# Stores of layer 1's preparation moved from the SP queue to the POOL queue in a two-layer decoder step

## Chip, cores and metric

The kernel runs on one core of a Trainium2 chip. The metric is the device time of one execution in microseconds; the median of three runs is given. The core has a matrix engine (TensorE, "PE" in the profile, with its weight loads as "PEld"), a vector engine (VectorE, "DVE"), a scalar engine (ScalarE, "ACT"), a general engine (GpSimd, "POOL") and a sequencer for transfers (SyncE, "SP"). Transfers run on 16 DMA engines.

## What is computed

One inference step of a two-layer decoder trunk over 1024 prompt rows and 8 x 4 sample rows (1056 columns of 1024 features). Layer 0 has a state-space branch and an HGRN2 branch. Layer 1, the one that the change touches, is RWKV-7 time mixing:

```python
xr, xw, xk, xv, xa, xg = (xn + xx * mix[m] for m in range(6))
r = xr @ wp[0]; k = xk @ wp[1]; v = xv @ wp[2]; z = xg @ wp[3]
decay = exp(-DECAY_SCALE * sigmoid(w0 + tanh(xw @ w1) @ w2))
a = sigmoid(a0 + (xa @ a1) @ a2)
g = sigmoid(xg @ g1) @ g2
kk = normalised heads of k * k_k;  k = k * (1 + (a - 1) * k_a)
# per head, token after token:
s = s * w_t - (s @ kk_t) outer (kk_t * a_t) + v_t outer k_t;  y_t = s @ r_t
out = (groupnorm(y) + bonus) * g * silu(z);  h = h + out @ w_o
```

A last RMSNorm gives the output.

## The kernel before

The columns are worked on in two halves (512 prompt columns; 512 prompt columns and 32 sample columns), features in eight blocks of 128 partitions ("pairs" of two heads). All dense products split their float32 operands into a high and a low part (`split`, L70 and L72) and run three matmuls per product (`dense2`, L805).

Layer 1 of one half goes through these steps. `l1_first` makes k, r and v (and, in `lora_second`, sw and a), block after block, and stores each to HBM (tensors kd, rd, vd, swd, ad; v also in chunks of 64 tokens, vc). `rwkv_ready` drives the preparation of the eight pairs: `rwkv_pre` loads k, sw and a of a pair, scans, and makes the operands ZB, which it stores to zr and bk; `rwkv_r` loads r, completes zr and stores rk; `rwkv_mask` makes masked products of the operands and stores them to nd; after four pairs `rwkv_inverse` loads nd back as sN in another layout, solves 31 steps on VectorE in the tile sX, and stores the inverses to xd and, transposed, to xnd. `l1_gate` makes the gates and `gates` stores two factors (g1, g2) by chunk. Then `chains` goes through 32 batches (two halves, eight chunks of 64 tokens, two groups of four pairs): `batch_load` loads BK, ZR, v, DT (from xd) and DA (from xnd), and `batch_products` (L1514), `batch_below` (L1548), `batch_block` (L1560) and the following steps compute; `rwkv_tail` loads the gates, and `l1_out` makes the output projection.

Nearly every transfer of the kernel is issued through the helper `dma` (L52), that is, on SP, loads and stores in one order. The generators above are interleaved by the rates in `run`; the order of the instructions on each engine's queue is then set, when the kernel is built, by a planner that places each instruction by priority and by estimated costs. Each engine, SP and POOL among them, works through its queue in that order. ZB, sN and sX have one buffer each. POOL's own work in these steps is small: the first column of each chunk in ZB (L1344), products for the samples (L1366), the clearing of sX ahead of an inverse (L1399), and parts of the normalisation (L857 to L863) and of the splits (L979, L980).

Of the kernel before, what the change touches and what calls it, by code (L numbers as in the profile page):

```python
# [25 lines left out]
NP = 4  # L26
# [10 lines left out]
class Builder:  # L37
# [12 lines left out]

    def dma(self, out, in_):
        self.nc.sync.dma_start(out, in_)  # L52

    def lnexp(self, after):

        with self.tc.issue_after(after.ins):
            self.nc.scalar.preload_act_table_set("natural_log_exp_and_others")
# [978 lines left out]
    def l1_first(self, hf):  # L1036

        nc, I, V, A = self.nc, self.I, self.nc.vector, self.nc.scalar
        c0, n, cuts = HALF[hf]
        cs = slice(c0, c0 + n)  # L1040

        lo = self.evt("lora")
        parts = self.lora_weights((("w", 1), ("a", 4)))
        xs = self.plain(hf), self.difference(hf)

        def first(ps, q0, q):
            A.activation(lo[0:64, q0:q0 + q], ps[0:64], AF.Tanh)
            A.activation(lo[64:128, q0:q0 + q], ps[64:128], AF.Copy)

        self.dense2(list(zip(parts, xs)), cuts, first)  # L1050
        yield

        wa = self.pair(n)
        for x, h, l in ((wa[0], slice(0, 64), slice(64, 128)), (wa[1], slice(64, 128), slice(0, 64))):
            A.activation(x[h, :n], lo[h, :n], AF.Copy)
            V.tensor_tensor(out=x[l, :n], in0=lo[h, :n], in1=x[h, :n].bitcast(F32), op=ALU.subtract)
        early = 0 if hf else self.ahead
        ready = self.rwkv_ready(hf, early)
        for j, m, dst, name in ((1, 2, self.k_d, "k"), (0, 0, self.r_d, "r"), (2, 3, self.v_d, "v")):
            self.wpool = self.wp8[hf][name]  # L1060
            self.evto = self.ev8[hf]
            xs = self.mixed(hf, m)
            for t in range(KT):
                while name == "k" and t > 3 and self.ah is None:
                    yield
                w = self.weights2(I["rw_w_rkvz"][0, j, :, 128 * t:128 * t + 128], KT)
                ev = self.evt()
                self.dense2([(w, xs)], cuts, lambda ps, q0, q: self.evac(ev[:, q0:q0 + q], ps, q, self.evto), last=t == KT - 1)
                self.dma(dst[t][:, cs], ev[:, :n])
                if name == "v":  # L1070
                    self.dma(self.vc_d[hf][t // NP][:, :, t % NP], ev[:, 0:512].rearrange("p (c t) -> p c t", t=64))
                if name == "k":
                    self.key_sums(hf, t, ev[:, :n])
                    if t == 3:
                        self.key_norms(hf)
                    elif t > 3 and early:
                        next(ready)
                else:
                    with self.tc.high_priority(offset=0):
                        next(ready, None)  # L1080
                if name == "v":
                    self.made["v"][hf] += 1
                yield
                if name == "k":
                    for i in range(2):
                        if t == self.lt[i]:
                            yield from self.lora_second(hf, wa, 4 * i)

    def lora_second(self, hf, wa, m0):

        nc, I, A = self.nc, self.I, self.nc.scalar
        c0, n, cuts = HALF[hf]
        cs = slice(c0, c0 + n)
        fs = slice(128 * m0, 128 * m0 + 512)
        wh, wl = self.weights2([I[x][0][:, fs] for x in ("rw_w2", "rw_a2")], KT)
        for m in range(4):
            both = [(slice(r0, r0 + 64), 4 * i + m, bias, dst, name, self.evt()) for i, r0, bias, dst, name in
                    ((0, 0, self.w0, self.sw_d, "sw"), (1, 64, self.a0, self.a_d, "aa"))]
            for q0, q in cuts:
                pss = [x[:, :q] for x in (self.bank(), self.PS(512))]  # L1100
                for x, ps, (rs, k, *_) in zip(wa, pss, both):
                    nc.tensor.matmul(ps, wh[:, k], x[:, q0:q0 + q], start=True, stop=False)
                for x, ps, (rs, k, *_) in zip(wa, pss, both):
                    nc.tensor.matmul(ps, wl[rs, k], x[rs, q0:q0 + q], start=False, stop=True)
                for ps, (rs, k, bias, dst, name, ev) in zip(pss, both):
                    A.activation(ev[:, q0:q0 + q], ps, AF.Sigmoid, bias=bias[:, m0 + m:m0 + m + 1])  # L1106
            for rs, k, bias, dst, name, ev in both:
                self.dma(dst[m0 + m][:, cs], ev[:, :n])
            if (m0 + m) % self.ly == self.ly - 1:
                yield  # L1110

# [69 lines left out]
    def gates(self, hf, p, g):  # L1181


        V, A = self.nc.vector, self.nc.scalar
        c0, n, cuts = HALF[hf]
        bon, v = (self.stage(x, 544)[:, :n] for x in ("ek", "es"))
        for t, d in ((bon, self.rk_d), (v, self.v_d)):
            self.dma(t, d[p][:, c0:c0 + n])
        self.within(n, cuts, bon, self.blkr, lambda cs, ps: V.tensor_tensor(out=v[:, cs], in0=v[:, cs], in1=ps, op=ALU.mult))
        V.scalar_tensor_tensor(out=v, in0=v, scalar=self.rwv["ln_b"][:, p:p + 1], in1=g, op0=ALU.add, op1=ALU.mult)  # L1190
        A.activation(bon, g, AF.Copy, scale=self.rwv["ln_w"][:, p:p + 1])
        for t, d, ds in ((bon, self.g1_d, self.g1s_d), (v, self.g2_d, self.g2s_d)):
            self.dma(d[hf][:, :, p], t[:, 0:512].rearrange("p (c t) -> p c t", t=64))
            if hf:
                self.dma(ds[:, p], t[:, 512:544])


    def rwkv_constants(self, kp):
# [96 lines left out]
    def rwkv_pre(self, hf, p, ahead=False):  # L1295
# [8 lines left out]
        c0, n, cuts = HALF[hf]  # L1304
        gs = slice(c0, c0 + n)
# [7 lines left out]
        ZB = T("ZB", 8, 3, 64)  # L1313
# [3 lines left out]
        for q0, q in cuts:  # L1317
            cs = slice(q0, q0 + q)
# [9 lines left out]
        P = sw  # L1328
# [12 lines left out]
        for x, d, z in ((pr(t1), pr(P), ZB[:, :, 0]),) + (((sm(t1), sm(P), sm3(SM[:, 0])),) if hf else ()):  # L1341
            c = x.shape[2]
# [4 lines left out]
        A.activation(a, a, AF.Identity, scale=c1(W["k_a"]), bias=c1(self.omka))  # L1347
        V.tensor_tensor(out=k, in0=k, in1=a, op=ALU.mult)
        both(V, k, t3, ZB[:, :, 2], 4)
        self.dma(self.zr_d[hf][p // NP][:, :, p % NP, 0], ZB[:, :, 0])  # L1350

        bk = self.bk_d[hf][p // NP][:, :, p % NP]
        self.dma(bk[0:64], ZB[0:64, :, 1:3])
        for i in range(2):
            self.dma(bk[64:128, :, i], ZB[64:128, :, 2 - i])
        return (p, ZB, a), (p, k, P)

    def rwkv_r(self, hf, p, k, P):

        V, G = self.nc.vector, self.nc.gpsimd  # L1360
        c0, n, cuts = HALF[hf]
        gs = slice(c0, c0 + n)
        r = self.stage("er", 544)[:, :n]
        self.dma(r, self.r_d[p][:, gs])
        if hf:
            G.tensor_tensor(out=self.SM[p][:, 1], in0=r[:, 512:544], in1=P[:, 512:544], op=ALU.mult)  # L1366
        V.tensor_tensor(out=P[:, 0:512], in0=r[:, 0:512], in1=P[:, 0:512], op=ALU.mult)
        self.dma(self.zr_d[hf][p // NP][:, :, p % NP, 1], P[:, 0:512].rearrange("p (c t) -> p c t", t=64))
        V.scalar_tensor_tensor(out=r, in0=r, scalar=self.rwv["r_k"][:, p:p + 1], in1=k, op0=ALU.mult, op1=ALU.mult)
        self.dma(self.rk_d[p][:, gs], r)  # L1370

    def rwkv_mask(self, hf, p, ZB, t1):

        nc, V = self.nc, self.nc.vector
        ps = self.PS(8, 32)
        for c in range(8):
            for i in range(2):
                js = slice(32 * i, 32 * i + 32)
                for h in range(2):
                    o, hr = 64 * h + 32 * i, slice(64 * h, 64 * h + 64)  # L1380
                    nc.tensor.matmul(ps[o:o + 32, c], ZB[hr, c, 1, js], ZB[hr, c, 0, js], start=True, stop=True)
        Nt = t1[:, 0:256].rearrange("p (c t) -> p c t", t=32)
        V.tensor_tensor(out=Nt, in0=ps, in1=self.cmd[:].unsqueeze(1).broadcast_to([128, 8, 32]), op=ALU.mult)
        self.dma(self.n_d[hf][p // NP][:, :, p % NP], Nt)

    def blocks(self, d, i, h):

# [3 lines left out]
    def rwkv_inverse(self, hf, b):  # L1391
# [3 lines left out]
        N, X = T("sN", 32, 32), T("sX", 32, 32)  # L1395
# [8 lines left out]
        with self.tc.high_priority(offset=0):  # L1404
            for j in range(31):
                n = 31 - j
                for E, t, s0, s1 in groups:
                    m = min(j + 1, s1) - s0
# [4 lines left out]
                for E, t, s0, s1 in groups:  # L1413
                    m = min(j + 1, s1) - s0
# [1 line left out]
                        w = t[:, 0:m * n].rearrange("p (s t) -> p s t", t=n)  # L1416
                        E.tensor_tensor(out=X[:, s0:s0 + m, j + 1:32], in0=X[:, s0:s0 + m, j + 1:32], in1=w, op=ALU.subtract)  # L1417
        for i, h, q in quarters:
            self.dma(self.blocks(self.x_d[hf][b][:, :, :, 32 * i:32 * i + 32], i, h), X[q])
        Xn = T("sN", 32, 32)  # L1420
        A.activation(Xn[:64], X[:64].rearrange("q s t -> q t s"), AF.Copy)
        for h in range(2):
            self.dma(self.xn_d[hf][b][:, h].rearrange("t c p s -> (c p) t s"), Xn[32 * h:32 * h + 32])

    def chains(self):

# [587 lines left out]
```

## Time and profile before

| what | us |
|---|---|
| median of three runs | 1889.67 |
| lowest, highest | 1886.45, 1898.71 |
| the profiled execution, its own time | 1892.82 |
| its span in the profile | 1891.1 |
| TensorE busy | 1706.0 |
| VectorE busy | 1297.9 |
| ScalarE busy | 977.1 |
| POOL busy | 140.7 |

The span goes from the first to the last instruction; the execution's own time is a little longer. Busy times count computing instructions alone; what an engine spends on issuing a transfer appears in the timeline of its queue ("SPq"). A row of a wait names the waiting instruction by its line and the tile that it makes, and what ended the wait.

### The profile page before, as it was taken

The numbers are of one execution on the slowest core, as the hardware profiler recorded it, in microseconds if no ns is written. First come the engines' busy times: TensorE is split into PE (matmuls) and PEld (weight loads), VectorE is DVE, ScalarE is ACT, GpSimd is POOL, SyncE is SP. The second block draws the span as 40 slices with busy tenths as digits, with TensorE's granted clock in tenths as the row PEclk, the third lists the DMA queues.
The fourth block names the chain that finished last, engine by engine and source line by source line (L and its number), as shares of the span: only waits on it lengthen the run. The fifth ranks groups of instructions, "written<-read, shape, count | busy, mean of one in ns | idle before, by whom it ended". The sixth has DMA issues, their size and how long they took to land. (4 is left out here: it accounts for less than half of the span.)

```text
span 1891.1 us, 39586 instructions
## 1 busy us (share of the span) xinstructions
PE 1706.0 (90%) x15060; PEld 1419.1 (75%) x15060; DVE 1297.9 (69%) x3010; ACT 977.1 (52%) x1886; POOL 140.7 (7%) x257
## 2 busy tenths in 40 slices
PE   4999989999997698997399999998899999999867
PEld 3877868988876576775377778887798887788756
DVE  5797798875678624789598734868968566565554
ACT  5445555555645334643356766645555435434454
POOL 1210011000004200011021000000000000000000
PEclk9899999888999797998599889989898998999799
DMA  8555554444562556699758234589794666453453
GB/s 205 173 157 141 136 149 130 138 131 123 172 186 84 173 184 200 185 255 262 194 141 203 81 125 161 146 226 243 206 220 120 178 159 166 126 157 104 118 157 106
DMA packets 555010, 308.39 MB, mean 163 GB/s; under 512 B 284883, under 2 KB 489043, under 8 KB 554820
## 3 DMA queue, kind: packets, MB, share of 16 engines
q1 hardware_dynamic: 554820, 305.86, 59.1%
q8 instruction: 119, 1.95, 0.4%
q14 instruction: 71, 0.58, 0.1%
HBM read 199.76 MB, written 104.81 MB: 161 GB/s over the span
## 5 line engine op out<-in xcount | busy, mean ns | idle before, releaser
L805 PE MATMUL dps<-xh,wh 128*128 128x272 f32 (+3 forms) x1696 | 581.2, 349 | 55.3 <-ACT xh L70 22.3
L805 PE MATMUL dps<-xl,wh 128*128 128x272 f32 (+3 forms) x1696 | 582.6, 346 | 18.7 <-DVE xl L72 18.1
L805 PE MATMUL dps<-xh,wl 128*128 128x272 f32 (+3 forms) x1696 | 575.3, 342 | 4.8 <-DVE wl L72 4.7
L805 PEld LDWEIGHTS dps<-xh,wh 128*128 128x128 f32 x1696 | 330.9, 198 | 108.2 <-ACT xh L70 27.0
L805 PEld LDWEIGHTS dps<-xl,wh 128*128 128x128 f32 x1696 | 334.5, 198 | 60.9 <-DVE xl L72 28.1
L805 PEld LDWEIGHTS dps<-xh,wl 128*128 128x128 f32 x1696 | 335.0, 198 | 37.7 <-DVE wl L72 8.4
L70 ACT ACTIVATE wh<-ws 128x512 fp32r<-128x512 f32 (+1 forms) x336 | 195.9, 619 | 289.9 <-PE dps L805 198.8
L72 DVE TENSOR_TENSOR wl<-ws,wh 128x512 fp32r<-128x512 f32 (+1 forms) x336 | 224.1, 685 | 97.6 <-ACT wh L70 96.7
L1514 PE MATMUL m<-ZR,BK 64*128 64x128 f32 x512 | 62.8, 296 | 21.4 <-DMA ZR<-zr 20.6
L1514 PEld LDWEIGHTS m<-ZR,BK 64*128 64x128 f32 x512 | 54.0, 196 | 28.7 <-issue 14.3
L70 ACT ACTIVATE xh<-mm 128x256 fp32r<-128x256 f32 (+1 forms) x112 | 52.8, 481 | 37.5 <-DVE mm L929 19.7
L72 DVE TENSOR_TENSOR xl<-mm,xh 128x256 fp32r<-128x256 f32 (+1 forms) x112 | 55.6, 507 | 5.6 <-ACT xh L70 2.6
L805 PE MATMUL dps<-gh,wh 128*128 128x272 f32 (+1 forms) x176 | 55.8, 317 | 2.1 <-ACT ev L1106 1.1
L805 PE MATMUL dps<-gl,wh 128*128 128x272 f32 (+1 forms) x176 | 54.8, 312 | 1.4 <-DVE gl L72 1.4
L805 PE MATMUL dps<-gh,wl 128*128 128x272 f32 (+1 forms) x176 | 54.5, 310 | 0.1
L1411 DVE TENSOR_TENSOR sT<-sX,sN 128x31 f32<-128x31 f32 (+15 forms) x124 | 42.1, 339 | 11.9 <-DMA sN<-nd 10.2
L66 DVE COPY ev<-dps 128x272 f32<-128x272 f32 (+1 forms) x43 | 22.5, 526 | 40.2 <-PE dps L805 35.0
L64 ACT ACTIVATE ev<-dps 128x272 f32<-128x272 f32 (+1 forms) x65 | 29.3, 450 | 37.5 <-PE dps L805 37.1
L1571 PE MATMUL m<-ZM,DT 64*64 64x128 f32 x512 | 41.1, 291 | 2.4 <-DVE MR L1517 2.4
L1417 DVE TENSOR_TENSOR sX<-sX,sT 128x31 f32<-128x31 f32 (+15 forms) x124 | 42.0, 339 | 1.7
L863 POOL COPY edge<-h 128x1 f32<-128x1 f32 x8 | 27.1, 3392 | 182.6 <-DVE h L850 182.5
L805 PEld LDWEIGHTS dps<-gh,wh 128*128 128x128 f32 x176 | 35.1, 199 | 6.3 <-ACT ev L1106 1.6
(644 smaller groups left out, 3365.1 us busy)
## 6 DMA issues: line engine op xcount, KB each, us to landing
ws<-in_rw_w_rkvz SPq DMA_DIRECT2D x128, 256.0 KB, 4.2
ws<-in_even_w_in SPq DMA_DIRECT2D x96, 256.0 KB, 3.7
ws<-in_rw_w_o SPq DMA_DIRECT2D x48, 256.0 KB, 3.1
ws<-in_even_w_out SPq DMA_DIRECT2D x32, 256.0 KB, 3.8
BK<-bk SPq DMA_DIRECT2D x32, 256.0 KB, 4.4
ZR<-zr SPq DMA_DIRECT2D x32, 256.0 KB, 2.7
pr<-ev SPq DMA_DIRECT2D x20, 272.0 KB, 2.0
pr<-ev SPq DMA_DIRECT2D x20, 256.0 KB, 3.9
```

The source lines that it names most:

```text
L64: return self.nc.scalar.activation(out, in_, AF.Copy)
L66: return self.nc.vector.tensor_copy(out, in_)
L70: self.nc.scalar.activation(hi, x, AF.Copy)
L72: e.tensor_tensor(out=lo, in0=x, in1=hi.bitcast(F32), op=ALU.subtract)
L805: mm = lambda c0, n, i, u, k, v: self.nc.tensor.matmul(ps[c0], u[:, k, :], v[:, c0:c0 + n], start=i == 0, stop=i == len(terms) - 1)
L863: G.tensor_copy(self.edge[:, k:k + 1], x[:, 512:513])
L1411: E.tensor_tensor(out=w, in0=X[:, s0:s0 + m, j:j + 1].broadcast_to([128, m, n]), in1=N[:, j, j + 1:32].unsqueeze(1).broadcast_to([128, m, ...
L1417: E.tensor_tensor(out=X[:, s0:s0 + m, j + 1:32], in0=X[:, s0:s0 + m, j + 1:32], in1=w, op=ALU.subtract)
L1514: nc.tensor.matmul(f2(pm[h][:, q]), f2(BK[hr, q]), f2(ZR[hr, q]), start=True, stop=True)
L1571: nc.tensor.matmul(pd[hr, q], DT[hr, q], ZM[hr, q], start=True, stop=True)
```

## The change

A second helper, `store`, issues a transfer from POOL instead of SP. The stores of layer 1's preparation call it: k, r, v, sw and a, the chunks of v, the gates, zr, bk, rk, nd, xd and xnd. Loads, the chains' output and layer 0 stay with `dma`.

```diff
     def dma(self, out, in_):
         self.nc.sync.dma_start(out, in_)
+
+    def store(self, out, in_):
+
+        self.nc.gpsimd.dma_start(out, in_)
...
-                self.dma(dst[t][:, cs], ev[:, :n])
+                self.store(dst[t][:, cs], ev[:, :n])
                 if name == "v":
-                    self.dma(self.vc_d[hf][t // NP][:, :, t % NP], ev[:, 0:512].rearrange("p (c t) -> p c t", t=64))
+                    self.store(self.vc_d[hf][t // NP][:, :, t % NP], ev[:, 0:512].rearrange("p (c t) -> p c t", t=64))
...
             for rs, k, bias, dst, name, ev in both:
-                self.dma(dst[m0 + m][:, cs], ev[:, :n])
+                self.store(dst[m0 + m][:, cs], ev[:, :n])
...
         for t, d, ds in ((bon, self.g1_d, self.g1s_d), (v, self.g2_d, self.g2s_d)):
-            self.dma(d[hf][:, :, p], t[:, 0:512].rearrange("p (c t) -> p c t", t=64))
+            self.store(d[hf][:, :, p], t[:, 0:512].rearrange("p (c t) -> p c t", t=64))
             if hf:
-                self.dma(ds[:, p], t[:, 512:544])
+                self.store(ds[:, p], t[:, 512:544])
...
-        self.dma(self.zr_d[hf][p // NP][:, :, p % NP, 0], ZB[:, :, 0])
+        self.store(self.zr_d[hf][p // NP][:, :, p % NP, 0], ZB[:, :, 0])
 
         bk = self.bk_d[hf][p // NP][:, :, p % NP]
-        self.dma(bk[0:64], ZB[0:64, :, 1:3])
+        self.store(bk[0:64], ZB[0:64, :, 1:3])
         for i in range(2):
-            self.dma(bk[64:128, :, i], ZB[64:128, :, 2 - i])
+            self.store(bk[64:128, :, i], ZB[64:128, :, 2 - i])
...
-        self.dma(self.zr_d[hf][p // NP][:, :, p % NP, 1], P[:, 0:512].rearrange("p (c t) -> p c t", t=64))
+        self.store(self.zr_d[hf][p // NP][:, :, p % NP, 1], P[:, 0:512].rearrange("p (c t) -> p c t", t=64))
...
-        self.dma(self.rk_d[p][:, gs], r)
+        self.store(self.rk_d[p][:, gs], r)
...
-        self.dma(self.n_d[hf][p // NP][:, :, p % NP], Nt)
+        self.store(self.n_d[hf][p // NP][:, :, p % NP], Nt)
...
         for i, h, q in quarters:
-            self.dma(self.blocks(self.x_d[hf][b][:, :, :, 32 * i:32 * i + 32], i, h), X[q])
+            self.store(self.blocks(self.x_d[hf][b][:, :, :, 32 * i:32 * i + 32], i, h), X[q])
...
         for h in range(2):
-            self.dma(self.xn_d[hf][b][:, h].rearrange("t c p s -> (c p) t s"), Xn[32 * h:32 * h + 32])
+            self.store(self.xn_d[hf][b][:, h].rearrange("t c p s -> (c p) t s"), Xn[32 * h:32 * h + 32])
```

## Rows read from the trace of the kernel before

**Rows 1.** The page, busy time, share and instructions of each engine.
```profile
PE 1706.0 (90%) x15060; PEld 1419.1 (75%) x15060; DVE 1297.9 (69%) x3010; ACT 977.1 (52%) x1886; POOL 140.7 (7%) x257
```

**Rows 2.** Stretches: PE, PEld, DVE, ACT, POOL busy us; PE clock, DMA share, GB/s.
```profile
850.00:900.00 50.00, 37.97 (x261) 26.66 (x260) 45.26 (x101) 19.80 (x32) 7.86 (x14) 0.83 1.02 266
900.00:950.00 50.00, 22.21 (x235) 17.71 (x236) 30.86 (x68) 16.03 (x37) 1.11 (x2) 0.55 0.72 171
...
1300.00:1350.00 50.00, 41.51 (x586) 35.56 (x586) 49.03 (x131) 31.53 (x77) 2.75 (x6) 0.94 0.74 204
1350.00:1400.00 50.00, 50.00 (x536) 46.66 (x536) 31.90 (x81) 19.18 (x37) 4.10 (x5) 0.96 1.00 237
```

**Rows 3.** PE's timeline, 893 to 945 us: start, us, what, idle before, releaser.
```profile
903.80 3.06 PE L1514 MATMUL m<-ZR,BK 64*128 64x128 f32 x16 [9.71 <-DMA ZR<-zr]
...
919.61 0.81 PE L1548 MATMUL m<-DA,MZ 32*32 32x32 f32 x16 [8.62 <-DMA DA<-xnd]
...
932.61 3.06 PE L1514 MATMUL m<-ZR,BK 64*128 64x128 f32 x16 [10.87 <-DMA ZR<-zr]
```

**Rows 4.** SP's timeline, 889 to 918 us: start, us of issuing, what.
```profile
889.08 0.53 SPq L52 DMA_DIRECT2D bk<-ZB  x1
...
891.87 1.20 SPq L52 DMA_DIRECT2D bk<-ZB  x2
893.17 2.26 SPq L52 DMA_DIRECT2D nd<-ea  x1
...
898.01 0.42 SPq L52 DMA_DIRECT2D ZR<-zr  x1
...
899.96 4.90 SPq L52 DMA_DIRECT2D xd<-sX  x3
...
908.15 0.50 SPq L52 DMA_DIRECT2D xnd<-sN  x1
...
916.88 0.99 SPq L52 DMA_DIRECT2D DA<-xnd  x2
```

**Rows 5.** DMA issues from 850 to 900 us: count, KB each, median us to landing.
```profile
vc<-ev SPq DMA_DIRECT2D x7, 256.0 KB
vd<-ev SPq DMA_DIRECT2D x6, 256.0 KB, 3.7
...
bk<-ZB SPq DMA_DIRECT2D x6, 128.0 KB, 3.4
bk<-ZB SPq DMA_DIRECT2D x3, 256.0 KB, 4.5
zr<-es SPq DMA_DIRECT2D x2, 256.0 KB
rkd<-er SPq DMA_DIRECT2D x2, 256.0 KB
...
zr<-ZB SPq DMA_DIRECT2D x2, 256.0 KB, 3.4
...
nd<-ea SPq DMA_DIRECT2D x3, 128.0 KB, 4.5
...
xd<-sX SPq DMA_DIRECT2D x1, 128.0 KB
```

**Rows 6.** Issues by tensor over the run: ns of one, min/median/max; first and last.
```profile
L52 SPq DMA_DIRECT2D kd<-ev x16: 319/338/712, 652.2 to 1191.1; - x16
...
L52 SPq DMA_DIRECT2D zr<-ZB x16: 519/530/979, 746.5 to 1359.0; - x16
```

**Rows 7.** POOL's groups: busy us, mean ns of one; idle before them, releasers.
```profile
L863 POOL COPY edge<-h 128x1 f32<-128x1 f32 x8 | 27.1, 3392 | 182.6 <-DVE h L850 182.5
L199 POOL COPY us<-ev 128x512 f32<-128x512 f32 x8 | 10.8, 1364 | 57.3 <-DVE ev L66 26.1 <-ACT ev L64 25.3 <-DVE ep L256 3.9
L1344 POOL COPY ZB<-e 128x8 f32<-128x8 f32 x16 | 8.5, 529 | 273.2 <-DVE e L1322 183.8 <-DMA bk<-ZB 20.6 <-DMA nd<-ea 19.6
```

**Rows 8.** POOL's clearing of sX: ns of one, min/median/max.
```profile
L1399 POOL MEMSET sX<- x4: 952/953/954, 640.3 to 1385.1; 128x1024 f32 x4
```

## The prediction

> **What bounds the kernel now.** I read the page's busy shares first, then the stretches of layer 1, then the waits of TensorE, then SP's own timeline, and last POOL's rows. TensorE is busy for 1706.0 of 1891.1 us, POOL for 140.7 [rows 1]. So a change that computes nothing can win only the time in which TensorE stands still, 185 us in all, and only the part of it that hangs on the moved stores. The stretches say where that is [rows 2]: from 850 to 900 us TensorE is idle for 12.0 us and from 900 to 950 for 27.8, at a granted clock of 0.83 and 0.55; from 1300 to 1350 it is idle for 8.5. Those are the places where the preparation of a half of layer 1 ends and the chains begin (first half) or run beside it (second half). In 850 to 900 and in 1350 to 1400 the 16 DMA engines are busy all the time (1.02 and 1.00), so there it is not SP alone that is late.
>
> The three long idles of TensorE in the first of these places are named by the trace [rows 3]: 9.71 us until the chains' first ZR load lands, 8.62 until DA lands, 10.87 until a ZR load of the second group lands; together 29.20. SP's own timeline [rows 4] shows what stood ahead of these loads. SP works one instruction after another, and from 889 to 917 it has hardly a gap: the ZR load is issued at 898.01 behind bk stores of 0.53 and 1.20 us (this one two stores) and an nd store of 2.26; the inverse's four xd stores go out from 899.96, the second xnd store at 908.15, and the DA load that needs it at 916.88, with zr, bk and rkd stores in between.
>
> **The change part by part.** *Removed from SP.* The diff moves 280 stores. By their access patterns 112 go out in 128 pieces, one per partition (k, r, v, sw, a: 80; rk: 16; the samples' gates: 16), 48 in 512 (bk), and 120 in 1024 (zr 32, gates 32, vc 16, nd 16, xd 16, xnd 8). The median issue on SP was 0.338 us for the first kind and 0.530 for the last [rows 6], so SP gets back about 112 x 0.338 + 168 x 0.530 = 127 us, spread over 650 to 1570 us. TensorE is covered by its own work nearly everywhere there, so I cost this at nothing except at the three idles:
> - first ZR load: bk 0.53 + 1.20 and nd 2.26 = 3.99 us stood right ahead of it; minus 4.0.
> - DA load: 8.7 us pass between the second xnd store and DA's issue; the moved stores among them leave, but xnd must still land before DA goes, and xd and xnd themselves become dearer (below). Of the 8.62 I take 2.5 back.
> - second ZR load: it waits for a zr store whose data are late themselves; SP is free for the er load ahead of that. I take 2.
>
> Of the 8.5 us in the second half, where chains and dense products both feed TensorE, I take 1.5. Sum: minus 10.
>
> *Added on POOL.* The trace shows no store issued by POOL, so its price is bounded by rows. The lower end is what SP needs for the same store, 0.53 us [rows 6]. How POOL makes the list of a store's pieces no row shows; if it goes through them one by one, its own work per element is the nearer row: a MEMSET of 1024 columns takes 0.953 us [rows 8], a COPY of 512 columns 1.364, so 2.7 for 1024 [rows 7]; the upper end that I can reason for is the 3.4 us to which a tiny COPY was stretched [rows 7], on top of the 0.5. I take the middle between MEMSET and COPY, 1.8 us for 1024 pieces, as 0.6 fixed and 1.2 for the pieces: 1.2 us for 512 and 0.75 for 128. In all 120 x 1.8 + 48 x 1.2 + 112 x 0.75 = 358 us of POOL, on an engine that is idle for long spells ahead of its ZB copies (273.2 us in all) [rows 7]. The tight stretch is 850 to 900: 32 moved stores [rows 5], 15 of 1024 pieces, 9 of 512, 8 of 128, together 27.0 + 10.8 + 6.0 = 43.8 us, and POOL's own 7.9 [rows 2]: 51.7 in 50. POOL just keeps up, each store some 1 to 3 us later than SP had it done.
>
> *Who waits for that.* POOL runs in order too. Behind a store that waits for its data stand POOL's ZB copies, the SM products and the clearing of X ahead of an inverse; behind the ZB copy stand the mask matmuls and the next stores; and VectorE can't write ZB for the next pair until bk has landed. The idle ahead of the ZB copies covers a microsecond or two per pair; if it is gone, VectorE stops, and with it the weight splits that TensorE needs. The four xd and two xnd stores cost 6 x 1.8 = 10.8 us where SP took from 899.96 to 908.65, 8.7; that is plus 2 at the DA load, which with the gain above is why I take only 2.5 there. For the rest I take plus 2.
>
> Sum: minus 10 plus 2 = minus 8 against the profiled execution's own 1892.82. That one is 3.15 above the median of the three runs, so the forecast is 1889.67 - 8 = 1882. The order of the instructions on each engine is planned anew when an instruction changes engine, so a few microseconds either way belong to the result whatever the stores do.
>
> The trace shows POOL's work stretched by its neighbour: a COPY of one column takes 3.4 us on average at one place [rows 7]. The Trainium skill (SBUF — State Buffer, section "SBUF: two separate sides") goes further: an issue on POOL writes its list through ports that VectorE can lock, and the DMA then waits; by it the queue on POOL would be the dearer one. But POOL's write-only MEMSET takes 952 to 954 ns in all four places [rows 8], so I give that rule a small chance, below. The same skill (DMA: Bandwidth & Descriptors, section "Latency and other measured facts") prices the first byte at about 1 us from POOL and 0.6 from SP; by that each step store-to-load is 0.4 later and the sum would be minus 7.
>
> **The rivals.**
> *A. SP's queue was all of it.* If POOL's store costs 1 us or less for 1024 pieces, nothing is late on POOL, and loads no longer stand behind stores. Then most of the 29.20 us goes, say 22, and 6 of the 8.5 in the second half: 1889.67 - 28 = 1862. For it: SP without a gap at the very place [rows 4]. Against it: the DMA engines are full there [rows 2], and a load that leaves SP sooner still waits for them.
>
> *B. POOL becomes the bound: slower.* The stretch of 850 to 900 decides. 15 x 1024 + 9 x 512 + 8 x 128 is 20.5 times 1024 pieces; with 0.6 fixed, 32 x 0.6 + 20.5 b = 50 - 7.9 gives b = 1.1, so from about 1.7 us per store of 1024 pieces on POOL runs behind (the forecast's 1.8 by 2 us, 2.4 by 14). At 3.9 (0.8 + 3.1 b) the stretch holds 32 x 0.8 + 20.5 x 3.1 = 89 us of stores, 39 too many; X, zr and xnd go out that much later, TensorE has nothing else there (27.8 us idle already), and the time is 1889.67 + 40 = 1930. For it: the COPY's 2.7 us lies well over the point from which this decides [rows 7]. Against it: MEMSET's 0.953 [rows 8].
>
> *C. The ports starve POOL.* If each of the 32 stores is stretched to 3.4 us more, as the COPY was, that is 109 us in 50 us: 60 late, 1950. This is the skill's rule worked out in rows; against it stands rows 8.
>
> *D. Nothing happens.* The DMA engines carry the same bytes, and they are the wall at 1.02 [rows 2]: 1890. The Trainium skill says so in general (DMA: Bandwidth & Descriptors, section "Issuing engines are not separate DMA queues"): only the time to issue is saved.
>
> **How the numbers follow.** Chances: forecast 0.36, A 0.29, B 0.25, C 0.06, D 0.04. A measurement of this kernel tells about 1% (19 us) from no change. The forecast's own range is 1870 to 1905; of its 0.36, 0.05 lies below 1871 and 0.03 above 1908. Of A 0.26 is faster by over 1%, of B 0.24 slower, C is slower, D within. Together faster 0.31, within 1% 0.36, slower 0.33. The range goes from 1852 (leaves 0.05 of A out) to 1945 (leaves C and 0.07 of B out). Cases of both signs hold most of the chance, so the likeliest one's range stands beside it: 1870 to 1905.
>
> **What would show it.** Right: POOL's store of 1024 pieces between 1.4 and 2.2 us; TensorE's three idles down from 29 to some 20 us; SP with gaps between 890 and 917. A shows as a price under 1 us and idles under 10 us. B shows as POOL without a gap from 850 to 930, ZB waits on VectorE for bk, and an idle of 30 us or more before the first DA or ZR; C as the same with store times that vary with VectorE's work. D shows as SP free, DMA engines at 1.0, idles as before. I am wrong in the mechanism if the idles change little and the time moves by over 1% elsewhere, for example in the gate stage or by another order of TensorE's work.

## The result and the profile after

The changed kernel is slightly slower: 1911.08 us median of 11 executions (1895.85 to 1919.15) against 1897.55 of 11 of the kernel before. The ratio on record, which here and below is not simply that of the two medians, is 1.0064 (95% interval 1.0038 to 1.0090). Measured once more on another occasion it was 1.0072 (1.0037 to 1.0106). The forecast was 1882, slightly faster. The profiled execution of the changed kernel took 1911.55 us, its span is 1909.8, 18.7 us more than before. Of these TensorE is busy for 12.3 more, with the same instructions, and idle for 6.4 more; the granted clock of the profiled executions is 0.900 on average, 0.911 before.

POOL did what the diff says: 280 more instructions, and a queue of its own. First the page of the changed kernel, busy times [rows 1] and queues (packets, MB, share of the 16 engines):

```profile
PE 1718.3 (90%) x15060; PEld 1430.2 (75%) x15060; DVE 1302.0 (68%) x3010; ACT 979.4 (51%) x1888; POOL 345.0 (18%) x537
...
q1 hardware_dynamic: 388548, 245.02, 45.3%
q0 software_dynamic: 19328, 60.84, 11.7%
```

The price of a store on POOL, ns of one (min/median/max), first and last start [rows 6 had SP's]:

```profile
L56 POOL DMA_DIRECT2D kd<-ev x16: 542/542/753, 654.4 to 1211.0; - x16
L56 POOL DMA_DIRECT2D bk<-ZB x48: 649/687/1264, 751.0 to 1397.8; - x48
L56 POOL DMA_DIRECT2D zr<-ZB x16: 847/865/1125, 749.2 to 1393.5; - x16
L56 POOL DMA_DIRECT2D xd<-sX x16: 786/790/817, 903.7 to 1490.2; - x16
```

So the median is 0.54 to 0.63 us for 128 pieces (0.63 for the samples' gates alone), 0.69 for 512 and 0.79 to 0.91 for 1024. All of them together are 345.0 - 140.7 = 204 us, and POOL is nowhere full. The stretches, in the columns of [rows 2]:

```profile
850.00:900.00 50.00, 43.52 (x350) 31.98 (x348) 45.61 (x100) 18.53 (x32) 32.40 (x44) 0.89 0.92 273
900.00:950.00 50.00, 20.33 (x223) 16.97 (x224) 31.13 (x78) 17.89 (x39) 12.99 (x18) 0.53 0.75 195
1300.00:1350.00 50.00, 46.24 (x604) 40.91 (x603) 44.51 (x115) 30.40 (x75) 15.42 (x24) 0.86 0.79 218
```

TensorE idles 6.5 us instead of 12.0 in the first of them, 29.7 instead of 27.8 in the second, and 3.8 instead of 8.5 in the third. Its three idles at the chains' start [rows 3] are now

```profile
902.16 3.06 PE L1518 MATMUL m<-ZR,BK 64*128 64x128 f32 x16 [3.00 <-DMA ZR<-zr]
...
920.94 0.28 PE L1552 MATMUL m<-DA,MZ 32*32 32x32 f32 x2 [6.00 <-DMA DA<-xnd]
...
933.61 3.06 PE L1518 MATMUL m<-ZR,BK 64*128 64x128 f32 x16 [10.03 <-DMA ZR<-zr]
```

together 19.03 us instead of 29.20: 10.2 less, where the forecast's three parts took 8.5 off them. (The other 14 of the DA matmuls wait for 0.42 more.) Yet the time is longer. What is late in these stretches is the stores themselves; DMA issues of the changed kernel from 850 to 900 us, median us to landing in the last column [rows 5]:

```profile
vd<-ev POOLq DMA_DIRECT2D x6, 256.0 KB, 6.3
...
zr<-ZB POOLq DMA_DIRECT2D x3, 256.0 KB, 6.3
bk<-ZB POOLq DMA_DIRECT2D x6, 128.0 KB, 7.3
...
nd<-ea POOLq DMA_DIRECT2D x3, 128.0 KB, 7.5
```

From SP these took 3.7, 3.4, 3.4 and 4.5 us. And something else has changed that the diff does not name: with the stores on another engine the planner ordered every engine anew. Of the program's 10,805 matmuls (15,060 instructions in the profile's count) 4,129 stand at another place than before, of ScalarE's 1,742 operations 696, of VectorE's 3,010 operations 1,236.

### The profile page after: what moved, and what is told of

It is laid out like the page before. It is cut to its first block, busy times and chain, and to the rows that moved or that the text cites. A ratio compares the mean times of both kernels' runs of the same rounds, so it can differ in the third digit from the quotient of the medians.

```text
span 1909.8 us, 39764 instructions
## 1 busy us (share of the span) xinstructions
PE 1718.3 (90%) x15060; PEld 1430.2 (75%) x15060; DVE 1302.0 (68%) x3010; ACT 979.4 (51%) x1888; POOL 345.0 (18%) x537
## 3 DMA queue, kind: packets, MB, share of 16 engines
q1 hardware_dynamic: 388548, 245.02, 45.3%
q0 software_dynamic: 19328, 60.84, 11.7%
## 5 line engine op out<-in xcount | busy, mean ns | idle before, releaser
L809 PE MATMUL dps<-xh,wh 128*128 128x272 f32 (+3 forms) x1696 | 580.4, 349 | 57.1 <-ACT xh L74 19.4
L1518 PE MATMUL m<-ZR,BK 64*128 64x128 f32 x512 | 67.4, 308 | 13.0 <-DMA ZR<-zr 13.0
L68 ACT ACTIVATE ev<-dps 128x272 f32<-128x272 f32 (+1 forms) x65 | 29.2, 451 | 37.3 <-PE dps L809 33.0
L1415 DVE TENSOR_TENSOR sT<-sX,sN 128x31 f32<-128x31 f32 (+15 forms) x124 | 41.9, 338 | 8.6 <-DMA sN<-nd 6.8
L1421 DVE TENSOR_TENSOR sX<-sX,sT 128x31 f32<-128x31 f32 (+15 forms) x124 | 41.9, 338 | 2.3 <-DVE sT L1415 0.4
L56 POOL DMA_DIRECT2D kd<-ev x16 | 8.9, 558 | 178.3 <-ACT ev L68 60.8
```

The costliest lines, as they stand in the source:

```text
L68: return self.nc.scalar.activation(out, in_, AF.Copy)
L809: mm = lambda c0, n, i, u, k, v: self.nc.tensor.matmul(ps[c0], u[:, k, :], v[:, c0:c0 + n], start=i == 0, stop=i == len(terms) - 1)
L1415: E.tensor_tensor(out=w, in0=X[:, s0:s0 + m, j:j + 1].broadcast_to([128, m, n]), in1=N[:, j, j + 1:32].unsqueeze(1).broadcast_to([128, m, ...
L1518: nc.tensor.matmul(f2(pm[h][:, q]), f2(BK[hr, q]), f2(ZR[hr, q]), start=True, stop=True)
```

## The experiments

Two theories remained: the **queue** (stores on POOL land later, and buffers and loads wait for them) and the **order** (the new plan makes TensorE wait elsewhere). A third, **scatter**, had to be watched: executions of one kernel differ by over 1%, and the granted clock goes with it. The first two can be taken apart, since a program's instructions are recorded in the same sequence whatever issues the stores. The kernel is recorded twice; the planned order of the first recording is laid on the second by edges that fix only the order of issue on an engine and wait for nothing (lines of e1's kernel):

```diff
     def store(self, out, in_):
-        self.nc.gpsimd.dma_start(out, in_)
+        (self.nc.gpsimd if self.on_pool else self.nc.sync).dma_start(out, in_)
...
+def follow(tc, order):
+
+    place = {n: k for k, n in enumerate(order)}
+    mine = {}
+    for i in tc.nc.cur_bb.bb.instructions:
+        if i.name in place and str(i.engine).split(".")[-1] in ('PE', 'Activation', 'DVE', 'Pool', 'SP'):
+            mine.setdefault(i.engine, []).append(i)
+    info = mybir.DependencyInfo(mybir.DependencyClass.NoSync, mybir.DependencyReason.DATA)
+    for ins in mine.values():
+        ins.sort(key=lambda i: place[i.name])
+        for a, b in zip(ins, ins[1:]):
+            tc.add_manual_dep(b, a.name, info, reason="order")
...
+    traced(first, inputs, False)
+    nc = bacc.Bacc("TRN2", target_bir_lowering=False, num_devices=1)
+    arrays = traced(nc, inputs, True, order_of(first))
```

All ratios are to the kernel before on the same chip; each is from 10 to 12 executions.

| run | order | issued by POOL | ratio (95% interval) |
|---|---|---|---|
| changed kernel | new | all 280 | 1.0064 (1.0038, 1.0090) |
| e14 (again) | new | all 280 | 1.0072 (1.0037, 1.0106) |
| e2 | new | none | 1.0059 (1.0027, 1.0092) |
| e1 | old | all 280 | 1.0044 (1.0016, 1.0071) |
| e12 (e1 again) | old | all 280 | 1.0001 (0.9970, 1.0032) |
| e4 | old | all but gates | 1.0005 (0.9984, 1.0025) |
| e7 | old | all but inverses | 1.0006 (0.9979, 1.0033) |
| e10 | old | all but both | 0.9970 (0.9943, 0.9997) |
| e15 (e10 again) | old | all but both | 1.0001 (0.9977, 1.0024) |
| e11 | old | gates and inverses | 0.9995 (0.9962, 1.0027) |
| e5 | old | gates | 1.0000 (0.9971, 1.0029) |
| e3 | planned for it | the 16 of rk | 1.0000 (0.9970, 1.0030) |
| e6 | new, one place edited | all 280 | 1.0012 (0.9986, 1.0038) |
| e13 | new, two places edited | all 280 | 1.0035 (1.0003, 1.0067) |
| e9 | new, one place edited | all but gates | 0.9983 (0.9955, 1.0010) |
| e8 | new, one place edited | none | 1.0032 (1.0009, 1.0055) |
| e16 | old, the same place spoiled | none | 1.0027 (1.0000, 1.0054) |

**e1, e2: the queue with the old order, the order with the old queue.**

> The stores are on POOL's queue as in the changed kernel, but every engine is held to the order of instructions that the kernel before has (its 10,805 matmuls, 1,742 ScalarE and 3,010 VectorE operations, and SP's loads). Queue theory (the time is lost because stores on a second queue land later, and the buffers and loads behind them are late): the ratio to before stays at 1.004 to 1.010, as the changed kernel's. Order theory (the time is lost because all instructions were planned anew when the stores changed their engine, and the new order makes TensorE wait elsewhere; the queue itself costs nothing and gives the 7 us at the chains' start): the loss is gone, ratio 0.994 to 1.000, and TensorE's idles at the chains' start are some 22 us or less instead of 29.

> The stores are on SP's queue as in the kernel before, but every engine is held to the order of instructions that the changed kernel has. Queue theory: the loss goes with the POOL queue, ratio 0.996 to 1.002. Order theory: the loss stays and the gain at the chains' start is missing, ratio 1.006 to 1.013, with an idle of about 5 us of TensorE at about 754 us behind ScalarE's exponentials, as in the changed kernel.

Both lost: 1.0044 and 1.0059. The second is, but for 0.0001, what the order theory asked for: with every store on SP and only the order changed, nearly the whole loss is there, and so is the idle behind ScalarE:

```profile
763.52 0.79 PE L810 MATMUL dps<-xh,wh 128*128 128x512 f32 x1 [5.22 <-ACT ev L1111]
```

The first seemed to say that the queue costs too, so the next runs looked for that.

**e3: another replanning.**

> Of all the stores only the 16 of the sums r (16 of 280 moved ones, small) are issued by POOL, in an order planned anew: 3,213 of the 10,805 matmuls stand at another place than before. Queue theory: 16 stores of 280 cost at most a twentieth of the loss, ratio 0.998 to 1.002. Order theory: any replanning can move the time by half a per cent either way, so a ratio as far from 1 as 0.993 or 1.008 would not surprise, and one within 0.998 to 1.002 would say that a replanning alone does not cost.

1.0000. A replanning that moves nearly a third of the matmuls need not cost anything; so it is this plan that costs, not replanning as such.

**e4, e5, e7, e10, e11: parts of the queue, old order.** The edit is `self.dma` instead of `self.store` in the lines of the stores that stay on SP; e4 for instance:

```diff
-            self.store(d[hf][:, :, p], t[:, 0:512].rearrange("p (c t) -> p c t", t=64))
+            self.dma(d[hf][:, :, p], t[:, 0:512].rearrange("p (c t) -> p c t", t=64))
             if hf:
-                self.store(ds[:, p], t[:, 512:544])
+                self.dma(ds[:, p], t[:, 512:544])
```

> All stores but the gates' 48 are issued by POOL, and every engine is held to the order of the kernel before. Gate theory (in the run with every store on POOL and the old order the gates' buffer came back later, so that ScalarE waited 2.9 us instead of 0.3 for the load of r*k at 960 to 1010 us, TensorE idled 3.9 us behind it, and its clock fell to 1.2 GHz): that wait is 0.3 to 1 us again, and with the shorter idles at the chains' start the ratio to before is 0.994 to 0.999. Landing theory (every store on the second queue lands later and what is lost is spread over the kernel): ratio 1.002 to 1.006. Scatter theory (the granted clock falls after any small idle, wherever it is): 0.998 to 1.004.

> Only the gates' 48 stores are issued by POOL, and every engine is held to the order of the kernel before. Gate theory: the wait for the load of r*k at 960 to 1010 us is 2 to 3 us, the idles at the chains' start are the 29 us of before, ratio 1.003 to 1.007. Landing theory: these stores are a sixth of those moved, ratio 1.000 to 1.002. Scatter theory: 0.998 to 1.003.

The wait named there behaves as the gate theory says, the time does not. Waits of ScalarE from 960 to 1015 us (us in total, times, longest), in e1, e4 and e5, and in e2:

```profile
ACT e L75 <- DMA ek<-rkd: 2.9, 3, 2.1
```

```profile
ACT e L75 <- DMA ek<-rkd: 0.3, 1, 0.3
```

```profile
ACT e L75 <- DMA ek<-rkd: 2.9, 2, 1.6
```

```profile
ACT e L75 <- DMA ek<-rkd: 5.7, 2, 4.7
```

With the gates alone on POOL the wait is 2.9 us as in e1, and costs nothing (1.0000). With every store on SP but the new order it is 5.7 us: in the changed kernel, which has 6.6, it comes from the order, not from the queue. The gate theory falls.

> Order of the kernel before on every engine; all stores issued by POOL, the gates' too, but for the 24 of the inverses (xd, xnd), which SP issues. Crowd theory (with every store on POOL the inverses' six stores leave at 986 to 991 us, 9 us earlier than from SP, while the gates' stores, their loads and the weights are under way; all then land late, and ScalarE waits for the load of r*k): without the inverses in the second queue the gates' stores come back in time, ratio 0.998 to 1.002, and ScalarE's wait for the load of r*k at 960 to 1015 us is under 1.5 us. Gate theory (gates' stores behind other stores of POOL are enough): ratio 1.003 to 1.006 and the wait 2 to 3 us. Scatter theory: 1.000 to 1.004.

e7: 1.0006. The crowd theory expected that, but the wait that it was to remove is 3.1 us: a miss in the mechanism.

> Order of the kernel before; POOL issues the operands of the chains (k, r, v, the decays, the masked products, their sums), while SP issues the gates and the inverses. Crowd theory (the loss with every store on POOL needs the gates and the inverses together on the second queue): at most what either alone gave back, ratio 0.997 to 1.001, with the three idles at the chains' start near 19 us. Landing theory (all stores on the second queue cost): 1.001 to 1.004. Scatter theory: 0.998 to 1.002 here, and the same for the two runs beside it.

> Order of the kernel before; POOL issues only the gates and the inverses, the other way round. Crowd theory: these two together cost by themselves what the whole queue cost with this order, and nothing is gained at the chains' start beyond what the inverses' earlier leaving gives: ratio 1.003 to 1.007. Landing theory: 1.000 to 1.003. Scatter theory: 0.998 to 1.002.

> Every store on POOL in the order of the kernel before, as in the first of these experiments (there 1.0044, interval 1.0016 to 1.0071), measured once more beside its two halves on one chip. If the loss is the queue's: 1.003 to 1.006 again. If the first measurement caught the granted clock low by chance: 0.998 to 1.002, as the runs without the gates or without the inverses, and then the queue as a whole costs and gives nothing that can be measured.

e10, e11 and e12: 0.9970, 0.9995, 1.0001. The crowd theory falls with e11. e12, the same kernel as e1 measured again on another chip, loses nothing; the two average 1.0022, and their intervals overlap. The executions of e1 had a mean granted clock of 0.9009, those of e12 of 0.9046 (the kernel before 0.9064 and 0.9063 beside them), and between executions of one kernel 0.001 of clock goes with 1.3 us (fitted over all runs of the study), so some 5 of the 8 us between the two means go with the clock. What lowered it in e1 is not known. The six measurements with the old order in which POOL issues the chains' operands (e1, e4, e7, e10, e12, e15) have a mean ratio of 1.0005. With the new order the queue makes as little difference: 1.0064 and 1.0072 on POOL, 1.0059 on SP. So the queue neither costs nor gives anything that can be measured here, which is to say about 0.2%. Nor do the edges themselves: e5 and e11 carry them at 1.0000 and 0.9995.

**e6, e8, e16: one place in ScalarE's order.** The clearest new idle of the changed kernel is at 755 us, long before the chains. ScalarE of the kernel before:

```profile
752.53 0.67 ACT L1106 ACTIVATE ev<-dps,w 128x512 f32<-128x512 f32 x1
753.22 1.28 ACT L1329 ACT_TABLE_LOAD   x1
754.51 0.63 ACT L1329 ACTIVATE as<-e 128x512 f32<-128x512 f32 x1
```

and of the changed kernel:

```profile
754.85 1.28 ACT L1333 ACT_TABLE_LOAD   x1
756.15 0.63 ACT L1333 ACTIVATE as<-e 128x512 f32<-128x512 f32 x1
756.81 0.63 ACT L1334 ACTIVATE e<-e 128x512 f32<-128x512 f32 x1
757.35 0.20 ACT L1335 ACTIVATE PC<-as 128x8 f32<-128x8 f32 x1
757.56 1.28 ACT L1110 ACT_TABLE_LOAD   x1
758.86 0.69 ACT L1110 ACTIVATE ev<-dps,w 128x512 f32<-128x512 f32 x1
```

The sigmoid that empties the bank of sums into which TensorE wants to write next (`lora_second`, the row with `ev<-dps,w`) stood ahead of the exponentials of `rwkv_pre`; now two exponentials, a small copy and two loads of a function table stand ahead of it. TensorE of the kernel before, of the changed one, of e6 and of e16 (start, us, what, idle before):

```profile
740.47 0.80 PE L1102 MATMUL dps<-xh,wh 128*128 128x512 f32 x1 [1.07 <-ACT ev L1106]
753.25 0.79 PE L805 MATMUL dps<-xh,wh 128*128 128x512 f32 x1 [1.09 <-ACT ev L1106]
```

```profile
742.67 0.79 PE L1106 MATMUL dps<-xh,wh 128*128 128x512 f32 x1 [1.07 <-ACT ev L1110]
...
759.60 0.80 PE L809 MATMUL dps<-xh,wh 128*128 128x512 f32 x1 [5.23 <-ACT ev L1110]
```

```profile
742.61 0.80 PE L1107 MATMUL dps<-xh,wh 128*128 128x512 f32 x1 [1.07 <-ACT ev L1111]
755.40 0.79 PE L810 MATMUL dps<-xh,wh 128*128 128x512 f32 x1 [1.09 <-ACT ev L1111]
```

```profile
742.47 0.80 PE L1107 MATMUL dps<-xh,wh 128*128 128x512 f32 x1 [1.07 <-ACT ev L1111]
759.58 0.80 PE L810 MATMUL dps<-xh,wh 128*128 128x512 f32 x1 [5.42 <-ACT ev L1111]
```

Between the same two matmuls 12.78 us pass in the kernel before, 16.93 in the changed kernel, 12.79 in e6 and 17.11 in e16. In e6 three instructions have moved in the new order, in e16 the same three in the old one, the other way. The edit of e6 (e8 and e9 have the same):

```diff
+EXPS, EVACS = ["I-8001", "I-8002", "I-8003"], ["I-7787", "I-7788"]
+
+
+def edited(order):
+
+    rest = [n for n in order if n not in EXPS]
+    b = rest.index(EVACS[-1])
+    return rest[:b + 1] + EXPS + rest[b + 1:]
```

> The changed kernel with its own order on every engine, but for three ScalarE instructions at about 755 us (two exponentials and a copy of 8 columns), which stand behind the two sigmoids that follow them instead of ahead of them. Order theory: TensorE's idle of 5.2 us there falls to about 1 us, and the time is 4 us (and some clock) below the changed kernel's: ratio to before 1.002 to 1.005. If ScalarE's order here is worth nothing, because what follows waits for the same stores: 1.006 to 1.007, as the changed kernel.

> All stores on SP as in the kernel before, the changed kernel's order on every engine, but for the three ScalarE instructions at about 755 us, which stand behind the two sigmoids. Order theory: the same swap gives back on SP what it gave on POOL (there 1.0064 became 1.0012), so the 1.0059 of the run with this order and all stores on SP becomes 1.000 to 1.003. If the swap's gain on POOL was of the POOL queue (the sigmoids' buffers wait for stores there): 1.004 to 1.007.

> The kernel before, all stores on SP and its own order on every engine, but for the three ScalarE instructions at about 755 us, which stand ahead of the two sigmoids as in the changed kernel's order. Order theory: TensorE idles about 5 us there instead of 1, the stretch that took 30.0 us takes 33 to 35 us, and the ratio to before is 1.002 to 1.005. If the place is worth its idle alone or less, because the chains' start 130 us later waits for SP's backlog all the same: the stretch takes 33 to 35 us and the ratio is 0.999 to 1.002.

e6: 1.0012, beside 1.0064 and 1.0072 without the edit; a little below the 1.002 expected. e8: 1.0032, beside e2's 1.0059; a little above the 1.003 expected. e16: 1.0027, as expected, though its interval (1.0000 to 1.0054) reaches into the other case's range; the three instructions are all that it changes. The three pairs say 0.3 to 0.6%; the rows say 4.1 us, 0.22%. With the new order, the three measurements that have the place as it is (the changed kernel twice, e2) average 1.0065, the four with it mended (e6, e8, e9, e13) 1.0016.

**e9, e13, e14: how much more is in the order.**

> The changed kernel in its own order with both edits: the three ScalarE instructions behind the two sigmoids, and the gates' 48 stores issued by SP. If the two losses are separate and each is where it was found: 0.995 to 0.999, below the kernel before, since the idles at the chains' start stay some 7 us shorter. If they are the same loss found twice, or what is left is scatter: 1.000 to 1.003.

> The changed kernel in its own order, with ScalarE's order mended at two places: the three instructions at about 755 us behind the two sigmoids, and at about 1,060 us the two copies of the chains' factors L ahead of the activations of the low-rank products, whose table loads they stood behind (TensorE idled 2.9 us there). Order theory: stretches of TensorE's idling of 5.2 and 2.9 us go, ratio to before 0.996 to 1.001, and 0.4 to 0.8% below the changed kernel beside it. Queue theory (what is left of the loss is the second queue's): 1.003 or more.

> The changed kernel as it is, measured once more beside the mended one. Order theory: 1.004 to 1.009 again. If the loss was chance, like that of the first run with the old order: 0.999 to 1.003.

> Order of the kernel before; only the chains' operands on POOL, measured once more. If the three idles' 10 us come through to the time at half their size, as the stretch from 885 to 960 us shows in the traces (70 to 71 us instead of 75): 0.996 to 0.999. If they are given back later: 0.999 to 1.002.

e14: the loss is real, 1.0072. Part of it goes with a lower granted clock: 0.9011 and 0.9002 on average in the two measurements of the changed kernel and 0.9031 in e2, against 0.9056, 0.9054, 0.9081 and 0.9051 in e6, e8, e9 and e13, and 0.9072 and 0.9074 in the kernel before beside e6 and e14; 0.006 goes with 8 us. Whether the idle pulls the clock down, no run tells: e16 has the same idle in the old order, and its clock is 0.9035 against 0.9044 beside it. e9: 0.9983, in its range, but ScalarE's wait for rkd is still 6.0 us with the gates on SP, so not for the reason given. e13: 1.0035, a miss. It lies in the range that was given for the queue, but it does not tell the two theories apart, since its second edit did not remove an idle but handed it on. In the changed kernel TensorE waits for a copy of L behind the low-rank activations, in e13 for the next copy, Y, in the same place:

```profile
1063.70 0.90 PE L1545 MATMUL m<-L,MZ 64*64 64x64 f32 x10 [2.94 <-ACT L L68]
```

```profile
1054.65 0.24 PE L1565 MATMUL m<-DT,Y 32*32 32x32 f32 x2 [3.12 <-ACT Y L69]
```

e6 and e13, which have the same mended place, average 1.0024 against 1.0068 of the two measurements of the changed kernel. e8's 1.0032 on SP says that the new order may cost at other places too. Two candidates, the rkd wait and the idle at L, are in its trace, and no run mended them; but e3 speaks against both. Its own plan has them as well (the second line is of its waits from 960 to 1015 us), not the idle at 755 us, and costs nothing (1.0000):

```profile
1045.90 0.90 PE L1545 MATMUL m<-L,MZ 64*64 64x64 f32 x10 [3.33 <-ACT L L68]
ACT e L74 <- DMA ek<-rkd: 7.3, 3, 3.0
746.51 0.79 PE L809 MATMUL dps<-xh,wh 128*128 128x512 f32 x1 [1.09 <-ACT ev L1110]
```

e15 did not repeat e10's gain: 1.0001. None of these versions is measurably faster than the kernel before.

**Where the 10 us of the three idles went.** Two distances between the same matmuls, in all the traces with the old order: from the matmul behind the sigmoid (753.25 in the kernel before) to the first ZR matmul (903.80), and from there to the first matmul of L846 behind the second group (944.52, L850 or L851 in the later kernels).

| old order | three idles, us | to first ZR, us | from there on, us |
|---|---|---|---|
| operands on SP: before, e5, e16 | 29.2, 28.9, 30.4 | 150.6, 148.2, 148.8 | 40.7, 41.5, 41.9 |
| operands on POOL: e1, e4, e7 | 19.2, 19.3, 19.5 | 145.8, 145.9, 144.9 | 39.3, 41.1, 40.8 |
| operands on POOL: e10, e12, e15 | 24.6, 21.3, 19.4 | 148.0, 147.9, 145.7 | 42.5, 39.5, 41.1 |
| operands on SP, gates and inverses on POOL: e11 | 23.9 | 147.6 | 38.4 |

With the operands on POOL the idles shrink by 29.5 - 20.5 = 9 us on average. Of that 149.2 - 146.4 = 2.8 us arrive at the first ZR load, and behind it little: 41.4 against 40.7. Together 3.5 us, 0.2% of the time, which is less than a measurement here can show. (Behind the first ZR load it matters more who issues the inverses: 39.6 us in the four traces where POOL does, e1, e4, e11 and e12, and 41.4 in the six others.) Two windows show where the rest stays. First the kernel before, then e15, over the same 220 matmuls:

```profile
903.80:944.52 40.72, 17.01 (x220) 15.11 (x220) 22.70 (x59) 10.82 (x30) 1.11 (x2) 0.54 0.80 187
```

```profile
898.53:939.65 41.12, 19.42 (x220) 16.38 (x221) 25.52 (x62) 13.30 (x34) 7.60 (x11) 0.50 0.76 186
```

TensorE idles 2.0 us less (21.7 instead of 23.7) and takes 2.4 us more for the same matmuls, at a granted clock of 0.50 instead of 0.54. The idle that is left is no longer the loads' alone. TensorE of e12 in that stretch, and below it the last wait of the same stretch in the kernel before:

```profile
891.34 3.06 PE L1519 MATMUL m<-ZR,BK 64*128 64x128 f32 x16 [7.03 <-DMA ZR<-zr]
899.07 1.79 PE L1546 MATMUL m<-L,MZ 64*64 64x64 f32 x16 [1.13 <-DVE L L71]
904.84 0.31 PE L1553 MATMUL m<-DA,MZ 32*32 32x32 f32 x2 [3.99 <-DMA DA<-xnd]
906.53 0.63 PE L1553 MATMUL m<-DA,MZ 32*32 32x32 f32 x14 [1.38 <-DMA DA<-xnd]
...
917.34 3.06 PE L1519 MATMUL m<-ZR,BK 64*128 64x128 f32 x16 [8.87 <-DMA ZR<-zr]
...
925.63 1.35 PE L1546 MATMUL m<-L,MZ 64*64 64x64 f32 x12 [0.61 <-DVE L L71]
930.82 2.18 PE L851 MATMUL dps<-e,ones 128*128 128x272 f32 x4 [3.84 <-DVE e L848]
```

```profile
944.52 2.18 PE L846 MATMUL dps<-e,ones 128*128 128x272 f32 x4 [3.83 <-DVE e L843]
```

New are the waits for L, VectorE's copies of the first products (1.13 and 0.61 us); the wait for e was there before. The second group's ZR load waits for data that come late whoever stores them (VectorE makes them at 923.48 us in the kernel before and at 908.52 in e12, both times behind the load of er): 8.87 us of 10.87 remain.

## Why the prediction was wrong

- **Price of a store on POOL: wrong, and it did not matter.** "I take the middle between MEMSET and COPY, 1.8 us for 1024 pieces"; it is 0.79 to 0.91, and all stores are 204 us, not 358. The nearest row was MEMSET's 0.953 [rows 8]. The upper end was misread: the 3.4 us of a one-column COPY [rows 7] are the mean of seven that took some 0.65 us and one that took 22.56 (min/median/max in ns in the line below). What held that one no run tells, so neither "stretched by its neighbour" nor the 3.4 us of rival C had a row behind them. Rivals B and C fall: POOL is busy for 32.4 of the 50 us of the tightest stretch, and a store's median there is within a fifth of its minimum for all tensors but rkd. The Trainium skill's rule that VectorE can lock POOL out of the ports by which it writes its lists (SBUF — State Buffer, section "SBUF: two separate sides") does not show here: VectorE is busy for 45.6 of these 50 us, and a vd store of 128 pieces still costs 0.562 us in the median and 0.642 at most. Whether VectorE's operations there are of the kind that the rule names, no run tells.

```profile
L863 POOL COPY edge<-h x8: 642/642/22558, 591.5 to 618.0; 128x1 f32<-128x1 f32 x8
```

- **Three idles: right, in the changed kernel partly by luck.** "TensorE's three idles down from 29 to some 20 us": 19.03. By parts the forecast was minus 4.0, 2.5 and 2; the changed kernel shows 6.7, 2.6 and 0.8. Most of the 6.7 is the new order's: in e2, with every store on SP, the first idle is 3.93 us instead of 9.71. With the old order and every store on POOL (e1, e12) the parts are 3.5 and 2.7, 4.5 and 3.3, 2.1 and 2.0, so the mechanism itself holds.
- **From idle to time: the term of the sum that was mis-sized.** "Sum: minus 10" took idle for time. With the order held, 9 us of idle were worth 2.8 us at the first ZR load and 3.5 at the end of that stretch, and the ratio of the whole is 1.0005: what remains is below what can be measured. The sum did not ask what is late next behind the loads: there were new waits for VectorE's copies, and the matmuls themselves took longer, at a lower clock.
- **The stores' later landing ("For the rest I take plus 2"): no cost shown.** They land some 3 us later in the full stretch (6.3 us instead of 3.4 for zr in the changed kernel, 5.9 and 5.7 with the old order in e1 and e12), and with the old order the time is 1.0044 and 1.0001 (e1, e12), 1.0000 for the gates (e5).
- **The order: the step that failed.** "The order of the instructions on each engine is planned anew when an instruction changes engine, so a few microseconds either way belong to the result" stood in the text but entered neither the sum nor a rival nor a chance. The sum put it at nothing. It decided: with all stores on SP this order costs 1.0059, and one place in it, shown from both sides (e6, e16), 4.1 us in the trace. The last sentence of the prediction came near ("by another order of TensorE's work"), but its sign was another one: idles that change little and a time that moves by over 1%. Here the idles went as forecast, the time moved by 0.6%, and the place that was found is in ScalarE's order, with TensorE waiting for it.
- **The base: scatter.** Of the 29 us between 1882 and 1911.08, 8 are the base: the forecast started from 1889.67, the median of three executions, and of eleven it is 1897.55. The rest is minus 8 forecast and about plus 12 measured.
- **Rival A** had the price right (under 1 us) and its consequence wrong: the idles did not fall under 10 us. **Rival D** was nearest for what the queue does to the time, though the idles did not stay as before. The Trainium skill has this as a rule (DMA: Bandwidth & Descriptors, section "Issuing engines are not separate DMA queues"): a second issuing engine saves only the time to issue. The old-order runs agree, with a mean of 1.0005.

What stays open: why the one place is worth 0.3 to 0.6% in the times and 0.22% in the rows, what lowers the clock, where the 0.1 to 0.2% lie that the new order still loses with the place mended, if they are no scatter, and whether the 3.5 us of the chains' start would show in a longer measurement.

## What to carry to other kernels

Moving a transfer to another engine can change the order of every engine when a planner orders the program, so compare the two orders first, and hold one of them fixed when you ask what the queue is worth. Ahead of a bank that TensorE waits for, an operation with another function table can cost ScalarE two loads: look for table loads in front of evacuations. And an idle removed is not time removed until the same distance between two matmuls is shorter; a ratio within 0.5% of 1 needs a second measurement before a cause is sought.

## What the runs showed of the hardware

- A store issued by POOL costs 0.542 us for 128 pieces (kd) and 0.865 for 1024 (zr) in the median, against 0.338 and 0.530 us on SP [rows 6]: dearer by 0.2 and some 0.34 us. The other work on the core stretches it little: every tensor's median over the run is within 8% of its minimum, and the longest single store took 1.36 us (nd).
- The profile counts POOL's queue with 19,328 packets for 60.84 MB. The kernel before has 554,820 packets on SP's queue, 166,272 more than the 388,548 that are left there, for the same 60.84 MB:

```profile
q1 hardware_dynamic: 554820, 305.86, 59.1%
```

The two queues together take 57.0% of the engines' span instead of 59.1. The bytes are the same; the packets of POOL's queue are fewer and larger, and its stores still land later in the full stretch.
- Measurements of one program differ, and the granted clock goes with it: e1 and e12 were 1.0044 and 1.0001, at mean clocks of 0.9009 and 0.9046. In e1's profile, from 1005 to 1015 us, TensorE was busy for 8.5 of 10 us at a granted clock of 0.66, so for most of it at the lower of its two levels (0.5, which is 1.2 GHz, and 1.0, which is 2.4), beside waits for ScalarE's evacuations of 3.9 us in all from 960 to 1015; the kernel before shows 1.00 all the way from 985 to 1050, with waits of 1.5. Scatter begins ahead of the change: the matmul that opens layer 1 (643.87 us in the kernel before) starts at 635.66 us in e12's profile and at 650.15 in e2's, before the first moved store.
- A load of a function table takes 1.28 us; two of them around three small operations held ScalarE for 4.0 us (754.85 to 758.86) and TensorE for 4.1.
